# A SwiGLU layer's stream from another queue, and its sums in the ring of the weights

## The chip, the cores and the metric

The kernel runs on one core of a Trainium2 chip. The metric is the device time of one execution in microseconds (us); the median of a few runs is taken. The engines are named as in the profile: PE is TensorE's matmul (PEld its weight load), DVE is VectorE, ACT is ScalarE, POOL is GpSimd, SP is SyncE, which issues most DMAs. Each engine works through its own instructions in order and waits on semaphores for the others.

## The reference

One encoder layer over 1024 positions of width 1024 in float32: a half-step SwiGLU, a mixing part (latent attention beside RWKV-7 heads), a second half-step SwiGLU and a norm. What the change touches is in the two SwiGLUs:

```python
h = x
u = modulate(rmsnorm(h, ffn1_norm_g[l]), sh1, sc1)
h = h + 0.5 * gt1[:, None, :] * swiglu(u, ffn1_w_gate[l], ffn1_w_up[l], ffn1_w_down[l])
...
def swiglu(u, w_gate, w_up, w_down):
    return (jax.nn.silu(u @ w_gate) * (u @ w_up)) @ w_down
```

The hidden width is 2816, which is 22 tiles of 128.

## The kernel before

**Products.** Each float32 operand is split into a high and a low part (`split`, L60): ACT copies the high one (L61), DVE subtracts it to get the low one (L62). A product is then three matmuls, high by high, high by low, low by high (`mm3`, L68), issued in that order, so the first two of a product need only ACT's copy and the third needs DVE's subtraction as well. Both parts of an operand lie in one tile `pair` of 4 KB per partition. The pairs of the weights come from a ring of eight tiles with the tag `"wo"`: the n-th takes the place of the (n-8)-th, and places are handed out in the order in which the Python code asks for them.

**The SwiGLU** (`ffn`) has two stages. The product up goes over the hidden tiles two at a time (f = 0, 2, ..., 20). For f of 2 and more, `products7` makes a 2x2 block product with seven products in place of eight, once for the gate and once for up: 2 x 7 products of 12 matmuls, 168 matmuls of 128x512 for each f. Between them DVE builds sums of weights (L376, L397), adds parts of results (L487, L492) and multiplies gate by up (L493), and ACT copies partial results out of PSUM (L390). The two hidden tiles `c` of an f go to DRAM (`hidD`, L497). From f = 4 on, `sums` also makes three differences of them, T3, T2 and T4, on DVE (L505: four subtractions, one of them in place on `c`), and stores them (`sumD`, L507). They need the result of the last of the f's fourteen products. The product down reads hidD and sumD back (`hraw`, L545), splits them, makes the seven products in groups (`seven_products`), and `give` (L560) adds each result to the stream `h`.

**The stream.** `h` is eight tiles d of 128 rows by two halves a of 512 positions, 256 KB each. During the product up its room is lent out: to the hidden tiles `c` (tags `h0_0` to `h6_0`), and to a ring of scratch tiles, `k.spare`, from which `tmp` takes in turn (T, t, part and hraw among others). At the turn from up to down the stream is read again, from `x` in the first SwiGLU (L1675, called from `turn`) and from `hD` in the second, by 16 DMAs on SP's queue, a = 0 first and d in order. `turn(-1)` comes before the last f and sets the scratch ring that this f and the product down use; `turn(0)` starts the stream's loads.

**Order.** A scheduler orders each engine's instructions from the code, within what tiles and semaphores allow. A tile that is asked for is given out only after all that was asked for before it in the same ring. While the first SwiGLU goes up, DVE also does `mod` steps (L140, L143, with weights `wmod`) and some `trig` steps, put in between the products.

Of the kernel before, what the change touches and what calls it, by code (L numbers as in the profile page):

```python
# [13 lines left out]
F32 = mybir.dt.float32  # L14
# [8 lines left out]
P = 128  # L23
D = 1024
S = 1024
HB = 512
ND = D // P
# [43 lines left out]
def banks(k, **names):  # L71

    for n, b in names.items():
        turn = itertools.cycle(b)
        k.bank.update((x, turn) for x in n.split("_"))
# [7 lines left out]
def tmp(k, name, n=HB, dt=F32):  # L83

    pool, tag, size = next(k.spare if n == HB else k.wide)
    return pool.tile([P, size], dt, name=name, tag=tag)[:, :n]


def spare(slots):

    return itertools.cycle([(*s, D)[:3] for s in slots])
# [196 lines left out]
def empty():  # L288
    return [[None, None] for _ in range(ND)]
# [13 lines left out]
def h_tiles(k, pool, a, out, singles=0):  # L303

    for d in range(singles):
        out[d][a] = pool.tile([P, HB], F32, name=f"h{d}_{a}", tag=f"h{d}_{a}")
    for d in range(singles, ND, 2):
        t = pool.tile([P, 2, HB], F32, name=f"h{d}_{a}", tag=f"h{d}_{a}")
        out[d][a], out[d + 1][a] = t[:, 0], t[:, 1]


def norm_raw(k, r, x, d, name, sh):

    nc = k.nc
    g, b = k.gs[name][:, d : d + 1], k.mod[:, sh, d : d + 1]
    if d % 2:
        nc.gpsimd.tensor_tensor(out=x, in0=x, in1=r[1], op=ALU.mult)
        nc.scalar.activation(out=x, in_=x, func=AF.Identity, scale=g, bias=b)
    else:
        nc.vector.scalar_tensor_tensor(out=x, in0=x, scalar=g, in1=r[0], op0=ALU.mult, op1=ALU.mult)  # L320
        nc.scalar.activation(out=x, in_=x, func=AF.Identity, bias=b)
# [42 lines left out]
def products7(k, pool, w, f, u, sink):  # L364


    nc = k.nc
    A = []
    for i in range(2):
        raw = pool.tile([P, 2, HB], F32, name="raw", tag="raw", bufs=4)  # L370
        nc.sync.dma_start(out=raw.rearrange("p a (d q) -> p (a d) q", q=P), in_=w[f + i])
        A.append((raw[:, 0], raw[:, 1]))
    (a11, a12), (a21, a22) = A

    def sub(x, y, out):
        nc.vector.tensor_tensor(out=out, in0=x, in1=y, op=ALU.subtract)  # L376
        return out

    def product(x, name, onto=None):
        hi, lo = pair(pool, "wo", 8)  # L380
        split(k, x, hi, lo)
        t = ps(k, "w7") if onto is None else onto
        for i in range(4):
            c = slice(i * P, (i + 1) * P)
            mm3(k, t, hi[:, c], lo[:, c], *u[name][i], onto is None and i == 0, i == 3, onto is not None)
        return t

    def kept(x):
        t = tmp(k, "part")
        nc.scalar.copy(out=t, in_=x)  # L390
        return t

    x = product(a11, "11")
    m1 = kept(x)
    yield
    s1 = pool.tile([P, HB], F32, name="s1", tag=next(k.s1))
    nc.vector.tensor_tensor(out=s1, in0=a21, in1=a22, op=ALU.add)  # L397
    y = product(s1, "T1")
    yield
    s3 = sub(a11, a21, a21)  # L400
    s2 = sub(s1, a11, a11)
    u2 = kept(product(s2, "T2", x))
    yield
    sink(0, 0, product(a12, "21"), m1)
    yield
    u3 = kept(product(s3, "T3", x))
    sink(1, 1, y, u3)
    yield
    sink(1, 0, product(a22, "T4"), u3)
    yield  # L410
    s4 = sub(a12, s2, a12)
    sink(0, 1, product(s4, "22", y), u2)
    yield
# [20 lines left out]
def ffn(  # L434
    k, u, h, wg, wu, wd, gt, pool, groups, cells, start, turn, steps1, steps2, final, done, pieces, ahead=None
# [6 lines left out]
    nc = k.nc  # L442
# [4 lines left out]
    def cell():  # L447
        where, tag = next(cells)
        return where.tile([P, 2, HB], F32, name="c", tag=tag)
# [31 lines left out]
    def up(f):  # L481

        c = [None, None]

        def silu(i, j, x, y):
            c[i] = cell() if c[i] is None else c[i]
            nc.vector.tensor_tensor(out=c[i][:, j], in0=x, in1=y, op=ALU.add)  # L487
            nc.scalar.activation(out=c[i][:, j], in_=c[i][:, j], func=AF.Silu)  # L488

        def gated(i, j, x, y):  # L490
            t = tmp(k, "t")
            nc.vector.tensor_tensor(out=t, in0=x, in1=y, op=ALU.add)  # L492
            nc.vector.tensor_tensor(out=c[i][:, j], in0=c[i][:, j], in1=t, op=ALU.mult)  # L493
            if (i, j) == (0, 1) and f >= NPL:
                sums()
            if (i, j) in ((1, 0), (0, 1)):
                nc.sync.dma_start(out=hidD[f + i], in_=c[i])  # L497

        def sums():

            (b11, b12), (b21, b22) = ((x[:, 0], x[:, 1]) for x in c)

            def sub(x, y, name=None):
                out = tmp(k, name) if name else x
                nc.vector.tensor_tensor(out=out, in0=x, in1=y, op=ALU.subtract)  # L505
                if name:
                    nc.sync.dma_start(out=sumD[name, f], in_=out)  # L507
                return out

            sub(b22, b12, "T3")  # L510
            t2 = sub(b22, sub(b12, b11), "T2")
            sub(b21, t2, "T4")

        return products7(k, pool, wg, f, u, silu), products7(k, pool, wu, f, u, gated)
# [1134 lines left out]
def tile_layer(ctx, tc, I, out):  # L1649
    k = Ctx()  # L1650
    setup(ctx, k, tc, I, out)
    nc = k.nc
# [10 lines left out]
    with pool_("ffn1") as pool:  # L1663
        fs = [(pool, f"f{i}") for i in range(12)]
        h0, h1 = [(pool, f"h{d}_0") for d in range(0, ND, 2)], [(pool, f"h{d}_1", HB) for d in range(6)]
        wide = [(pool, "e"), (pool, "h6_1")]
        k.wide = spare(us)
        k.spare = spare(fs[8:])
        h = empty()
        u = {}  # L1670

        def load_x(a):
            h_tiles(k, pool, a, h, 6 * a)
            for d in range(ND):
                nc.sync.dma_start(out=h[d][a], in_=I["x"][d, :, a * HB : (a + 1) * HB])  # L1675

        vectors(k, pool)
        load_x(0)
        early = 2
        slices = {}  # L1680
# [38 lines left out]
        def normed(a, r):  # L1719
            for d in range(ND):  # L1720
                if a == 0 and d >= early:
                    mods(d)
                norm_raw(k, r, h[d][a], d, "ffn1_norm_g", 0)
            return [h[d][a] for d in range(ND)]
# [4 lines left out]
        x = []  # L1729

        def first_half():
            spread_c(k, pool)
            load_mods(range(early, 4))
            load_x(1)
            load_mods(range(4, ND))
            x.append(normed(0, r0))
            stream_first(k, u, x[0], slots)
# [8 lines left out]

        def turn(g):
            if g < 0:
                k.spare = spare(wide + h1)
                return  # L1750
            if g == 0:
                banks(k, dn="67012345")
                for a in range(2):
                    load_x(a)
            if g == 3:
                banks(k, in0="012", dn_in1="34", in2="5", norm="67")
                k.spare = spare(fs[8:])
# [20 lines left out]
        def ahead(a, tiles):  # L1778
# [6 lines left out]
        ffn(  # L1785
            k, u, h, I["ffn1_w_gate"], I["ffn1_w_up"], I["ffn1_w_down"], k.mod[:, 2, :], pool, groups(fs, us),
            itertools.chain([wide[0], us[7]], itertools.cycle(h0)), (lambda: None, lambda: (first_half(), second_half()), lambda: None, both), turn, steps1, steps2,
            n2.final, n2.done, [(0, WHOLE), (1, WHOLE)], ahead,
        )
# [71 lines left out]
    h, y, u = empty(), empty(), {}  # L1861
    own = lambda name, side="right": ctx.enter_context(pool_(name, side))
    h0, h1 = [f"h{d}_0" for d in range(0, ND, 2)], [(f"h{d}_1", HB) for d in range(6)]
    up = Pools((own("u3b"), [f"u{i}" for i in range(8)]))
    pool = Pools((own("h2b"), h0), (own("w2"), ("raw", "f8", "f9", "f10", "f11", "nwy", "nwt")))
    us, fs = [(up, f"u{i}") for i in range(16)], [(pool, f"f{i}") for i in range(12)]
    h0, h1 = [(pool, t) for t in h0], [(pool, *t) for t in h1]
# [11 lines left out]
    es = [(pool, "e"), (pool, "e2")]  # L1879
    k.spare = spare(es)  # L1880
    slots = iter(fs + us)
    x = []

    def then(a, r):
        for d in range(ND):
            norm_raw(k, r, h[d][a], d, "ffn2_norm_g", 6)
        x.append([h[d][a] for d in range(ND)])
        if a == 0:
            stream_first(k, u, x[0], slots)
        else:  # L1890
            stream_second(k, u, x[1], us[8:])
# [14 lines left out]

    def turn(g):
        if g < 0:
            k.spare = spare(es + h1)
            return  # L1910
        if g == 0:
            banks(k, dn="67012345")
            for a in range(2):
                h_tiles(k, pool, a, h, 6 * a)
                for d in range(ND):
                    nc.sync.dma_start(out=h[d][a], in_=k.hD[a][:, d, :])
        if g == 3:
            banks(k, dn="670123", norm="45")
            k.spare = spare(us[8:])
# [61 lines left out]
```

## Time and profile before

| | |
|---|---|
| median of three runs | 2087.97 us (2081.59 to 2088.29) |
| profiled execution | 2091.08 us, its span 2089.0 us |
| mean granted clock of TensorE | 0.978 |
| PE busy | 1992.1 us, 95% of the span |
| DVE, ACT, POOL busy | 1542.5, 885.2, 242.0 us |
| matmuls of the product up (`ps_w`) | 3744, 873.8 us |

The span runs from the first to the last instruction. The granted clock is 1.00 where TensorE has its full 2.4 GHz and 0.50 where it has 1.2 GHz. A busy time counts an engine as busy while an instruction is in it; the mean duration of a single matmul (near 395 ns) is longer than the distance between two, since they are pipelined.

### The profile page before, as it was taken

What the parts mean: (1) busy time and instruction counts of PE and PEld (TensorE: products, weight loads), DVE (VectorE), ACT (ScalarE), POOL (GpSimd) and SP (SyncE); (2) the same over time, 40 slices, a digit from 0 to 9 for tenths busy, and PEclk for the clock granted to TensorE, in tenths of its full rate; (3) what the DMA queues carried; (4) which work ended last, traced back from release to release, by engine and by line L of the source; (5) the groups of instructions that cost most, each with busy time, mean ns of one, the idle gap of its engine ahead of it and who ended that gap; (6) DMA issues with size and microseconds to landing.
All of it is one profiled execution on the core that took longest, in us unless ns stands there. A gap on an engine that the chain in (4) does not pass through costs nothing.

```text
span 2089.0 us, 29462 instructions
## 1 busy us (share of the span) xinstructions
PE 1992.1 (95%) x10648; PEld 1605.8 (77%) x10648; DVE 1542.5 (74%) x2955; ACT 885.2 (42%) x1662; POOL 242.0 (12%) x271
## 2 busy tenths in 40 slices
PE   6999999998999999998988999899999999989998
PEld 4788888886888777766767787787888888868887
DVE  6999997668996577887655667567566656689975
ACT  5643334344443465543343434355333333344433
POOL 1100000000000244531141221111000000000001
PEclk8999999999999999999988999999999999999999
DMA  8277743246452124666347884741223323474412
GB/s 335 85 246 249 247 172 126 101 172 227 152 171 86 66 66 120 154 149 147 89 100 155 190 186 133 237 159 42 87 79 106 121 76 107 162 251 152 141 61 81
DMA packets 225681, 302.12 MB, mean 145 GB/s; under 512 B 104704, under 2 KB 138880, under 8 KB 225536
## 3 DMA queue, kind: packets, MB, share of 16 engines
q1 hardware_dynamic: 219600, 294.84, 45.3%
q0 software_dynamic: 1280, 3.15, 0.5%
q10 hardware_dynamic: 4656, 2.25, 0.4%
q8 instruction: 84, 1.38, 0.3%
q14 instruction: 61, 0.50, 0.1%
HBM read 216.81 MB, written 80.74 MB: 142 GB/s over the span
## 4 chain that ended last, share of the span: by engine, by line
PE 77%; DVE 12%; DMA 5%; issue 3%; ACT 2%; POOL 1%; SPq 1%; DVEq 0%; ACTq 0%; POOLq 0%
PE ps_w L68 39%; PE ps_dn L68 19%; PE ps_in L68 5%; PE ps_wo L68 4%; DVE pair L62 2%; PE ps_ov L1264 2%; PE ps_s L68 1%; DVE T L1359 1%; DVE Tpr L1355 1%; PE ps_z L1472 1%; PE ps_y L1506 1%; PE ps_pt L1256 1%; DVE wmod L140 1%; DMA hraw<-hidD 1%; DMA fD<-T 1%
## 5 line engine op out<-in xcount | busy, mean ns | idle before, releaser
L68 PE MATMUL ps_w<-pair 128*128 128x512 f32 x3744 | 873.8, 395 | 12.8 <-ACT pair L61 9.4
L68 PEld LDWEIGHTS ps_w<-pair 128*128 128x128 f32 x3744 | 704.6, 189 | 179.1 <-ACT pair L61 10.7
L68 PE MATMUL ps_dn<-pair 128*128 128x512 f32 x1512 | 357.5, 398 | 15.1 <-DVE h L560 11.8
L68 PEld LDWEIGHTS ps_dn<-pair 128*128 128x128 f32 x1512 | 287.7, 191 | 84.0 <-DVE h L560 13.5
L68 PE MATMUL ps_in<-pair,win 128*128 128x512 f32 x960 | 241.0, 403 | 2.6 <-ACT pair L282 2.2
L61 ACT CAST pair<-raw 128x512 fp32r<-128x512 f32 x256 | 153.6, 621 | 183.5 <-PE ps_w L68 98.2
L68 PEld LDWEIGHTS ps_in<-pair,win 128*128 128x128 f32 x960 | 179.5, 190 | 51.7 <-issue 10.4
L62 DVE TENSOR_TENSOR pair<-raw,pair 128x512 fp32r<-128x512 f32 x256 | 175.1, 696 | 38.8 <-ACT pair L61 38.7
L560 DVE SCALAR_TENSOR_TENSOR h<-ps_dn,mod,h 128x512 f32<-128x512 f32 (+1 forms) x208 | 148.7, 725 | 53.4 <-PE ps_dn L68 49.5
L390 ACT COPY part<-ps_w 128x512 f32<-128x512 f32 x120 | 70.4, 587 | 207.8 <-PE ps_w L68 196.7
L61 ACT CAST pair<-draw 128x256 fp32r<-128x256 f32 x216 | 80.1, 404 | 135.6 <-PE ps_dn L68 64.3
L61 ACT CAST pair<-hraw 128x512 fp32r<-128x512 f32 x142 | 86.1, 619 | 65.9 <-PE ps_dn L68 41.5
L62 DVE TENSOR_TENSOR pair<-hraw,pair 128x512 fp32r<-128x512 f32 x142 | 95.5, 683 | 11.8 <-ACT pair L61 11.4
L492 DVE TENSOR_TENSOR t<-ps_w,part 128x512 f32<-128x512 f32 x80 | 53.8, 685 | 56.9 <-ACT part L390 46.8
L208 POOL TENSOR_TENSOR nacc<-nacc,nsq 128x512 f32<-128x512 f32 x12 | 18.1, 1508 | 660.8 <-ACT nsq L204 660.8
L62 DVE TENSOR_TENSOR pair<-draw,pair 128x256 fp32r<-128x256 f32 x216 | 84.9, 416 | 11.5 <-ACT pair L61 11.4
L140 DVE SCALAR_TENSOR_TENSOR wmod<-wmod,cact 128x1024 f32<-128x1024 f32 x68 | 82.6, 1216 | 4.7 <-DMA wmod<-w_mod 4.7
L68 PE MATMUL ps_dn<-pair,dh 128*128 128x512 f32 (+1 forms) x320 | 83.8, 350 | 0.0
L487 DVE TENSOR_TENSOR c<-ps_w,part 128x512 f32<-128x512 f32 x80 | 53.4, 684 | 39.7 <-ACT part L390 33.5
L703 POOL TENSOR_TENSOR h<-h,nr 128x256 f32<-128x256 f32 (+1 forms) x6 | 5.4, 920 | 650.0 <-ACT nr L231 650.0
L68 PE MATMUL ps_wo<-pair,woh 128*128 128x512 f32 x256 | 80.6, 396 | 0.0
L488 ACT ACTIVATE c<-c 128x512 f32<-128x512 f32 x80 | 49.3, 631 | 31.6 <-DVE c L487 30.7
(349 smaller groups left out, 2798.6 us busy)
## 6 DMA issues: line engine op xcount, KB each, us to landing
wmod<-w_mod SPq DMA_DIRECT2D x68, 512.0 KB, 4.6
raw<-ffn_w_gate SPq DMA_DIRECT2D x44, 512.0 KB, 4.3
raw<-ffn_w_up SPq DMA_DIRECT2D x44, 512.0 KB, 4.3
hidD<-c SPq DMA_DIRECT2D x44, 512.0 KB, 3.3
draw<-ffn_w_down SPq DMA_DIRECT2D x44, 512.0 KB, 5.3
hraw<-hidD SPq DMA_DIRECT2D x72, 256.0 KB, 3.4
h<-x SPq DMA_DIRECT2D x32, 256.0 KB, 5.2
hD<-h SPq DMA_DIRECT2D x32, 256.0 KB, 2.0
```

The source lines that it names most:

```text
L61: k.nc.scalar.copy(out=hi, in_=src)
L62: k.nc.vector.tensor_tensor(out=lo, in0=src, in1=hi.bitcast(F32), op=ALU.subtract)
L68: k.nc.tensor.matmul(out, lhsT=x, rhs=y, start=start, stop=stop, skip_group_check=onto)
L140: k.nc.vector.scalar_tensor_tensor(out=w, in0=w, scalar=1.0, in1=k.cact, op0=ALU.mult, op1=ALU.mult, accum_out=m)
L390: nc.scalar.copy(out=t, in_=x)
L487: nc.vector.tensor_tensor(out=c[i][:, j], in0=x, in1=y, op=ALU.add)
L488: nc.scalar.activation(out=c[i][:, j], in_=c[i][:, j], func=AF.Silu)
L492: nc.vector.tensor_tensor(out=t, in0=x, in1=y, op=ALU.add)
L560: nc.vector.scalar_tensor_tensor(out=y, in0=x, scalar=gt[:, d : d + 1], in1=y, op0=ALU.mult, op1=ALU.add)
L1256: nc.tensor.transpose(tp[:, q : q + P], pr[:, s0 + q : s0 + q + P], k.ident)
L1264: nc.tensor.matmul(x.po[:, cols], lhsT=pt[:, b * P : (b + 1) * P], rhs=k.v[b][:, cols], start=b == 0, stop=b == x.i)
L1355: nc.vector.tensor_tensor(out=v, in0=T[:, t, 0:m][:, None, :].broadcast_to([P, n, m]), in1=xp[:, t, m:][:, :, None].broadcast_to([P, n, m] ...
```

## The change

Three edits in both SwiGLUs. The stream's 16 loads at the turn are issued from POOL, four tiles of d at a time, in the order (d 0, 1; a 0), (d 0, 1; a 1), (d 2, 3; a 1), (d 2, 3; a 0), then the same for d 4 to 7. T3, T2 and T4 no longer come from the scratch ring: for each f from 4 on `sums` asks the ring `"wo"` for two tiles of 4 KB, one for T3 and T2, one for T4. And the scratch ring of the last f and the product down takes the tiles of `h1` in another order.

```diff
+def stream_again(k, pool, h, src):
+
+    for a in range(2):
+        h_tiles(k, pool, a, h, 6 * a)
+    for q in range(0, ND, 4):
+        for i, a in ((0, 0), (0, 1), (2, 1), (2, 0)):
+            for d in range(q + i, q + i + 2):
+                k.nc.gpsimd.dma_start(out=h[d][a], in_=src(d, a))
...
             (b11, b12), (b21, b22) = ((x[:, 0], x[:, 1]) for x in c)
 
+            t, t4 = (pool.tile([P, 2, HB], F32, name="T", tag="wo", bufs=8) for _ in range(2))
+            place = {"T3": t[:, 0], "T2": t[:, 1], "T4": t4[:, 0]}
+
             def sub(x, y, name=None):
-                out = tmp(k, name) if name else x
+                out = place[name] if name else x
                 nc.vector.tensor_tensor(out=out, in0=x, in1=y, op=ALU.subtract)
...
             if g < 0:
-                k.spare = spare(wide + h1)
+                k.spare = spare(wide + [h1[i] for i in (4, 5, 0, 2, 3, 1)])
                 return
             if g == 0:
                 banks(k, dn="67012345")
-                for a in range(2):
-                    load_x(a)
+                stream_again(k, pool, h, x_half)
```

The second SwiGLU has the same edits, with `hD` in place of `x`. In the changed kernel the lines of the product up stand ten to thirteen further on: the multiplication by up is L503, the subtractions of T are L518.

**Between two f of the product up.** The rows below are PE's at the end of f = 12 of the second SwiGLU, and the same rows stand at each such place. A name is out<-in, `ps_w7` is a result in PSUM, `pair` the operands, and x3 means three matmuls in a row. Before, `ps_w7_14727` is the last product of f = 12:

```order
L68 MATMUL ps_w7_14910<-pair_12487,pair_14907 128x512 x2
L68 MATMUL ps_w7_14727<-pair_12870,pair_14819 128x512 x3
L68 MATMUL ps_w7_14727<-pair_12871,pair_14819 128x512 x3
L68 MATMUL ps_w7_14727<-pair_12872,pair_14819 128x512 x3
L68 MATMUL ps_w7_14727<-pair_12873,pair_14819 128x512 x3
L68 MATMUL ps_w7_14855<-pair_13102,pair_14890 128x512 x3
L68 MATMUL ps_w7_14855<-pair_13103,pair_14890 128x512 x3
L68 MATMUL ps_w7_14855<-pair_13104,pair_14890 128x512 x3
L68 MATMUL ps_w7_14855<-pair_13105,pair_14890 128x512 x3
L68 MATMUL ps_w7_14910<-pair_12487,pair_14907 128x512
```

The products 14910 and 14855 belong to the next f; 14910 has begun before the last product of f = 12 has. In the changed kernel the last product is `ps_w7_14714`, and nothing of the next f stands ahead of its end:

```order
L68 MATMUL ps_w7_14714<-pair_12863,pair_14806 128x512 x3
L68 MATMUL ps_w7_14714<-pair_12864,pair_14806 128x512 x3
L68 MATMUL ps_w7_14841<-pair_12474,pair_14838 128x512 x2
L68 MATMUL ps_w7_14861<-pair_13097,pair_14858 128x512 x2
L68 MATMUL ps_w7_14841<-pair_12474,pair_14838 128x512
L68 MATMUL ps_w7_14841<-pair_12475,pair_14838 128x512 x3
```

The next f now begins with two products of which two matmuls each (high by high, high by low) come first; the fifth matmul is the first that takes a low part, that of pair_14838.

At the same place DVE has these rows in the kernel before (`t` is the sum read from the last product's PSUM):

```order
L492 TENSOR_TENSOR t_14834<-ps_w7_14727,part_14757 128x512
L62 TENSOR_TENSOR pair_15024<-raw_14982,pair_15024 128x512
L493 TENSOR_TENSOR c_14641<-c_14641,t_14834 128x512
L505 TENSOR_TENSOR T3_14837<-c_14661,c_14641 128x512
L505 TENSOR_TENSOR c_14641<-c_14641 128x512
L505 TENSOR_TENSOR T2_14841<-c_14661,c_14641 128x512
L62 TENSOR_TENSOR pair_15041<-raw_14982,pair_15041 128x512
L505 TENSOR_TENSOR T4_14844<-c_14661,T2_14841 128x512
L487 TENSOR_TENSOR c_14923<-ps_w7_14910,part_14868 128x512
```

And in the changed kernel these:

```order
L502 TENSOR_TENSOR t_14821<-ps_w7_14714,part_14744 128x512
L503 TENSOR_TENSOR c_14628<-c_14628,t_14821 128x512
L518 TENSOR_TENSOR T_14824<-c_14648,c_14628 128x512
L518 TENSOR_TENSOR c_14628<-c_14628 128x512
L518 TENSOR_TENSOR T_14824<-c_14648,c_14628 128x512
L518 TENSOR_TENSOR T_14825<-c_14648,T_14824 128x512
L62 TENSOR_TENSOR pair_14838<-raw_14834,pair_14838 128x512
L62 TENSOR_TENSOR pair_14858<-s1_14856,pair_14858 128x512
```

The low part that PE's fifth matmul takes (pair_14838) has moved behind all of the sums; before, the low parts of the next f's first products stand ahead of them. This order holds at all 16 places between two f, eight in each SwiGLU (f = 4 to 18). At 13 of them DVE has just the seven instructions from `t` to that low part; in the first SwiGLU four, three and no `mod` multiplications and no, no and three `trig` steps stand among them at f = 4, 6 and 8.

**At the turn.** The same rows of the changed kernel at the end of f = 20 of the first SwiGLU; `hraw` are hidden tiles read back for the product down, and pair_3944 is the first weight of it, 256 wide:

```order
L502 TENSOR_TENSOR t_3836<-ps_w7_3635,part_3684 128x512
L62 TENSOR_TENSOR pair_4024<-hraw_4022,pair_4024 128x512
L62 TENSOR_TENSOR pair_4063<-hraw_4061,pair_4063 128x512
L503 TENSOR_TENSOR c_3702<-c_3702,t_3836 128x512
L62 TENSOR_TENSOR pair_4098<-hraw_4096,pair_4098 128x512
L518 TENSOR_TENSOR T_3839<-c_3741,c_3702 128x512
L518 TENSOR_TENSOR c_3702<-c_3702 128x512
L62 TENSOR_TENSOR pair_4131<-hraw_4129,pair_4131 128x512
L518 TENSOR_TENSOR T_3839<-c_3741,c_3702 128x512
L62 TENSOR_TENSOR pair_4136<-hraw_4134,pair_4136 128x512
L62 TENSOR_TENSOR pair_4172<-hraw_4170,pair_4172 128x512
L518 TENSOR_TENSOR T_3840<-c_3741,T_3839 128x512
```

The low part of pair_3944 is DVE's next row. PE has eight matmuls between the last product up and the first that takes this low part. Before, ten matmuls of the product down stand ahead of the last product up. The second SwiGLU's turn reads alike.

## Rows read from the trace of the kernel before

**Rows 1.** Busy time by stretch: us, PE, PEld, DVE, ACT, POOL, PEclk, DMA share, GB/s.
```profile
100.00:150.00 50.00, 50.00 (x220) 40.92 (x219) 47.26 (x94) 19.34 (x35) 0.00 (x0) 1.00 0.72 243
...
400.00:450.00 50.00, 50.00 (x220) 40.91 (x219) 32.67 (x52) 17.20 (x31) 0.00 (x0) 1.00 0.30 107
...
1550.00:1600.00 50.00, 50.00 (x217) 40.37 (x216) 30.54 (x48) 17.78 (x31) 0.00 (x0) 1.00 0.29 100
```

**Rows 2.** PE's matmuls of the product up by line, 100 to 450, then 1450 to 1850.
```profile
L68 PE MATMUL ps_w<-pair 128*128 128x512 f32 x1524 | 350.4, 392 | 0.2 <-ACT part L390 0.2
...
L68 PE MATMUL ps_w<-pair 128*128 128x512 f32 x1692 | 392.7, 393 | 0.0
```

**Rows 3.** DVE in order of time between two f: start us, us, what.
```profile
1577.12 0.68 DVE L492 TENSOR_TENSOR t<-ps_w,part 128x512 f32<-128x512 f32 x1
1577.72 0.68 DVE L62 TENSOR_TENSOR pair<-raw,pair 128x512 fp32r<-128x512 f32 x1
1578.32 0.69 DVE L493 TENSOR_TENSOR c<-c,t 128x512 f32<-128x512 f32 x1
1579.04 0.69 DVE L505 TENSOR_TENSOR T<-c 128x512 f32<-128x512 f32 x1
1579.77 0.69 DVE L505 TENSOR_TENSOR c<-c 128x512 f32<-128x512 f32 x1
1580.49 0.69 DVE L505 TENSOR_TENSOR T<-c 128x512 f32<-128x512 f32 x1
1581.10 0.68 DVE L62 TENSOR_TENSOR pair<-raw,pair 128x512 fp32r<-128x512 f32 x1
1581.70 0.68 DVE L505 TENSOR_TENSOR T<-c,T 128x512 f32<-128x512 f32 x1
```

**Rows 4.** DVE's groups, 100 to 480: count | busy us, mean ns | idle before.
```profile
L140 DVE SCALAR_TENSOR_TENSOR wmod<-wmod,cact 128x1024 f32<-128x1024 f32 x54 | 65.7, 1217 | 4.7 <-DMA wmod<-w_mod 4.7
...
L746 DVE SCALAR_TENSOR_TENSOR trig<-trig 128x512 f32<-128x512 f32 x20 | 13.4, 683 | 0.0
```

**Rows 5.** PE in order of time at the first turn: idle before it in brackets.
```profile
499.31 6.66 PE L68 MATMUL ps_dn<-pair 128*128 128x512 f32 x21 [3.34 <-DVE h L560]
510.49 4.84 PE L68 MATMUL ps_dn<-pair 128*128 128x512 f32 x13 [4.51 <-DVE h L560]
```

**Rows 6.** PE in stretches of one us behind the first of these: us, PE, PEclk, DMA.
```profile
500.00:501.00 1.00, 1.00 (x5) 0.75 1.01 414
501.00:502.00 1.00, 1.00 (x4) 0.50 1.02 410
502.00:503.00 1.00, 1.00 (x4) 0.50 0.95 240
503.00:504.00 1.00, 1.00 (x4) 0.54 0.81 274
504.00:505.00 1.00, 1.00 (x6) 1.00 1.00 383
```

**Rows 7.** The turns by stretch, columns as in the first group.
```profile
470.00:495.00 25.00, 25.00 (x111) 20.48 (x110) 24.11 (x49) 14.42 (x32) 0.00 (x0) 1.00 0.83 267
495.00:515.00 20.00, 12.15 (x39) 9.02 (x38) 14.69 (x30) 4.71 (x11) 0.00 (x0) 0.83 0.75 257
...
1860.00:1880.00 20.00, 12.76 (x41) 9.30 (x40) 13.90 (x29) 3.94 (x10) 0.00 (x0) 0.83 0.79 270
```

**Rows 8.** The chain that ended last, at the first turn: start us, us, what.
```profile
496.17 8.28 DMA T2D<-T
...
504.51 5.15 DMA h<-x
...
509.68 0.76 DVE h L560
```

**Rows 9.** DMA issues: queue, count, KB each, us to landing.
```profile
h<-x SPq DMA_DIRECT2D x32, 256.0 KB, 5.2
...
ybD<-lgx POOLq DMA_DIRECT2D x8, 256.0 KB, 4.2
```

More of the change, by code (lines that the diff above doesn't have):

```diff
@@ L1670, in tile_layer @@
         u = {}
+        x_half = lambda d, a: I["x"][d, :, a * HB : (a + 1) * HB]
         def load_x(a):
@@ L1674, in load_x @@
             for d in range(ND):
-                nc.sync.dma_start(out=h[d][a], in_=I["x"][d, :, a * HB : (a + 1) * HB])
+                nc.sync.dma_start(out=h[d][a], in_=x_half(d, a))
         vectors(k, pool)
@@ L1908, in turn @@
         if g < 0:
-            k.spare = spare(es + h1)
+            k.spare = spare(es + [h1[i] for i in (4, 5, 0, 2, 3, 1)])
             return
@@ L1912, in turn @@
             banks(k, dn="67012345")
[L1913 to L1916, printed above, removed]
+            stream_again(k, pool, h, lambda d, a: k.hD[a][:, d, :])
         if g == 3:
```

## The prediction, on record before the run

> **What bounds the kernel now.** The first view is busy time by stretch. Over both products up PE is busy 50.00 us of 50, with 217 to 220 matmuls and a granted clock of 1.00, while DVE stands between 30.5 us (second SwiGLU) and 47.3 us (first, with its mod steps) [rows 1]. The groups by line say the same from the other side: from 100 to 450 us PE was idle 0.2 us in 1524 matmuls, from 1450 to 1850 us 0.0 in 1692 [rows 2]. So these stretches, some 750 us of the span, are bound by PE alone, at 0.2273 to 0.2304 us a matmul (50 over 220 and 217), and an idle microsecond that is put into them is one more microsecond of the end. What the reader is to look for is therefore not busy time but whether PE still finds its next operand ready.
>
> The second view is PE in order of time at the turn from up to down. There it does wait: 3.34 us and 4.51 us in the first SwiGLU, for DVE's addition to the stream [rows 5], which the chain leads back to a load of the stream (5.15 us) and that to the store of T2 in a scratch tile on the stream's place (8.28 us) [rows 8]. In 20 us of the first turn PE is idle 20 - 12.15 = 7.9 us and the clock is 0.83, which is 0.17 x 20 = 3.4 us of full speed lost; in the second 7.2 and 3.4 [rows 7]. So the two turns lose 11.3 + 10.6 = 21.9 us together. That is all that the change can win there.
>
> **The change, part by part.**
>
> *T's room in the ring of the weights.* No operation is added: four subtractions, three stores as before. What changes is which of PE's operands must wait. The places of the ring are given out in the code's order, and the code asks for T's two tiles after the last product of an f and ahead of the next f's first weight. So a weight of the next f can't get its place before T has one, and the orders shown with the change are the result: the next f's first low part stands on DVE behind t, c, T3, c, T2 and T4, and t needs the end of the f's last product. Before, PE had begun the next f by then.
>
> The length of that chain is read from the same seven instructions of before [rows 3]. Where an instruction needs the one before it, starts lie 0.72 us apart (1578.32, 1579.04, 1579.77, 1580.49); where it doesn't, 0.60 (1580.49, 1581.10, 1581.70). From t to T4 are five such needs, 5 x 0.72 = 3.6; from T4 to the low part 0.60; it lasts 0.68: 4.9 us. For the hand-over from PE to DVE and back I add 0.1 each, an estimate after the one place where it shows (DVE's addition ends at 509.68 + 0.76 = 510.44, PE starts at 510.49 [rows 5, 8]). PE has four matmuls that need high parts only, 4 x 0.23 = 0.9. Idle: 4.9 + 0.2 - 0.9 = 4.2 us. Bounds: 3.5 if all starts lie 0.60 apart, 4.7 with hand-overs of 0.35.
>
> There are 16 such places. Thirteen have the bare chain: 13 x 4.2 = 54.6 us. At f = 4 and 6 of the first SwiGLU four and three mod multiplications of 1.22 us [rows 4] stand in the chain, and the others' starts are then 0.60 apart (4.3 in place of 4.9): 4.3 + 4 x 1.22 + 0.2 - 0.9 = 8.5 and 7.3. At f = 8 three trig steps of at most 0.68 [rows 4]: between 4.2 and 5.6, taken as 5.1. Idle in all: 75.5 us. Nothing gives it back, since PE alone bounds what follows.
>
> *The clock behind the idle time.* After the idle 3.34 us of the first turn, PE's next stretches of one us had granted clocks of 0.75, 0.50, 0.50 and 0.54, then 1.00 again [rows 5, 6]: the lower level, 1.2 GHz, for a loss of 0.25 + 0.50 + 0.50 + 0.46 = 1.7 us. The idle 4.2 us lies between that one and the 4.51 us, whose stretch counts 13 matmuls in its first 4.84 us [rows 5], where full speed has 21. So I charge 1.7 us at each of the 16 places: 27.2 us. The bound on the other side is nothing, if four matmuls and an idle stretch are not like a longer idle one.
>
> *The turn.* The last f's T delay the first weight of the product down as well. From t to its low part are thirteen DVE instructions, six of them splits of hidden tiles, so starts lie 0.60 apart: 12 x 0.60 + 0.4 (256 wide, taken as somewhat over half of 0.68) = 7.6, + 0.2, less eight matmuls, 1.8: 6.0 idle, and 1.7 for the clock. If the stream is there in time, this 7.7 us takes the place of 11.3 and 10.6: 6.5 us won in two turns. The new order and the scratch tiles are worth that only if T's stores no longer stand ahead of the loads, which holds: their tiles are not the stream's. Bounds: nothing won, or 21.9.
>
> *POOL's queue.* POOL is free (0.00 busy in all of these stretches [rows 1, 7]), so nothing is queued behind the loads that others wait for. A load from it has its row in ybD, as large, 4.2 us to landing against 5.2 for the stream's own [rows 9]; I cost it at nothing, up to 1 us either way.
>
> *The sum.* 75.5 + 27.2 - 6.5 = 96 us on the profiled 2091.1, so 2187; the median of the runs lies 3.1 below that execution, so 2184. Scheduling also shifts the mixing part's order a little; no row prices that, and I give it nothing, with some 6 us either way.
>
> **Rivals.**
>
> *The idle time doesn't bring the clock down* (0.14). For it: the four matmuls run in the middle of the wait. Against: the idle 3.34 us was enough [rows 5, 6]. Then 75.5 + 12.0 - 21.9 = 66 us: 2154.
>
> *The stream starves* (0.07). DVE is busy 24.11 us of the 25 before the turn [rows 7], and loads from POOL would wait for a free DVE, so behind the chain. 16 x 256 KB at the 410 GB/s of [rows 6] are 10.2 us, and with the clock 12 us more at each turn: 2208. Against it: ybD's 4.2 us. It decides only if the loads start after T4. The Trainium skill, "SBUF — State Buffer", in the box on the "DVE blocks DMA" trap, says that a DMA issued from GpSimd has its descriptors written by GpSimd, which a VectorE operation in a two-port mode locks out. That page speaks for this rival and against the change; the rows show no load from POOL beside a full DVE, so the trace doesn't settle it.
>
> *The change is a repair of the turn alone* (0.03): PE finds products to run while T is made, as before, and the stream is early. Then all that the turns lose is won: 2088 - 21.9 = 2066. It decides where DVE's chain ends ahead of PE's own work, under 0.9 us, and the chain is 4.9.
>
> *The loads win nothing* (in the forecast's 0.72): 2191.
>
> The rest (0.04) is what I don't see, in the mixing part above all.
>
> **How the numbers follow.** The likeliest is the sum, 2184 us (0.72; its own range 2170 to 2200, from 3.7 to 4.7 us of idle time a place and a turn between nothing and 12 us won). The range goes down to the rival without the clock and up to the one with the starved stream: 2150 to 2210. A time within 0.3% (6 us) can't be told from no change here. Slower by more: 0.95; faster: 0.03; within: 0.02.
>
> **What would show it.** In the trace after: PE idle 4 us before the first low parts of each f, ended by DVE's L62, 16 times, 3.5 to 5 us each and more at f = 4 and 6; stretches with a granted clock of 0.50 behind each; T3 to T4 on DVE directly before that L62; 217 to 220 matmuls in 50 us become some 190. At the turn: one wait of some 6 us for the first weight's low part in place of two for the stream. The prediction is wrong if PE has no such waits, if the clock stays at 1.00 behind them, or if PE waits for the stream's loads behind the turn.

## The result and the profile after

| | before | changed |
|---|---|---|
| median | 2086.16 us | 2253.36 us |
| span of the profiled execution | 2089.0 us | 2249.8 us |
| mean granted clock | 0.978 | 0.950 |

The ratio is 1.080 (95% interval 1.078 to 1.082): 8% slower, where 2184 us and at most 2210 were predicted. The sign and the place were right; the loss is 161 us of span where 96 were worked out.

PE in order of time over the first places between two f in the changed kernel (start us, us, instructions, idle before them and what ended it):

```profile
162.97 6.71 PE L68 MATMUL ps_w<-pair 128*128 128x512 f32 x28 [1.06 <-DVE c L497]
183.28 31.72 PE L68 MATMUL ps_w<-pair 128*128 128x512 f32 x128 [13.60 <-DVE pair L62]
217.50 7.38 PE L68 MATMUL ps_w<-pair 128*128 128x512 f32 x24 [2.49 <-DVE c L497]
228.00 5.54 PE L68 MATMUL ps_w<-pair 128*128 128x512 f32 x16 [3.13 <-DVE t L502]
244.27 37.61 PE L68 MATMUL ps_w<-pair 128*128 128x512 f32 x152 [10.73 <-DVE pair L62]
283.46 3.02 PE L68 MATMUL ps_w<-pair 128*128 128x512 f32 x12 [1.58 <-DVE t L502]
293.25 41.45 PE L68 MATMUL ps_w<-pair 128*128 128x512 f32 x172 [6.76 <-ACT pair L61]
338.80 41.58 PE L68 MATMUL ps_w<-pair 128*128 128x512 f32 x168 [4.09 <-DVE pair L62]
384.46 36.80 PE L68 MATMUL ps_w<-pair 128*128 128x512 f32 x152 [4.08 <-DVE pair L62]
422.71 3.95 PE L68 MATMUL ps_w<-pair 128*128 128x512 f32 x16 [1.46 <-DVE t L502]
...
573.53 121.89 PE L68 MATMUL ps_dn<-pair 128*128 128x512 f32 x522 [10.01 <-ACT pair L61]
```

Where before PE waited 0.2 us in all of this stretch [rows 2], it now waits once for each f. From f = 10 on the wait is 4.08 to 4.10 us, the bare one; so it is at all eight places of the second SwiGLU. In front of them stand 13.60, 10.73 and 6.76 us. And there are short waits for `t` or `c` inside an f, which the prediction did not have. The last row is the turn: 10.01 us.

The groups by line of the changed kernel (busy, mean ns, idle before, releasers) give the sum:

```profile
L68 PE MATMUL ps_w<-pair 128*128 128x512 f32 x3744 | 921.4, 408 | 117.1 <-DVE pair L62 80.3
...
L68 PE MATMUL ps_dn<-pair 128*128 128x512 f32 x1512 | 354.4, 396 | 20.3 <-ACT pair L61 20.2
```

The product up has 117.1 us of idle time where it had 12.8, and its matmuls take 921.4 us where they took 873.8: 104.3 + 47.6 us. The product down adds 5.2 of idle time (20.3 against 15.1) less 3.1 of busy (354.4 against 357.5). That is 154.0 of the span's 160.8; the rest, 6.8, lies in the mixing part, which the change doesn't touch, and in the ends.

One bare wait as DVE saw it, the end of an f in the second SwiGLU of the changed kernel:

```profile
1812.28 0.69 DVE L502 TENSOR_TENSOR t<-ps_w,part 128x512 f32<-128x512 f32 x1 [1.37 <-PE ps_w L68]
1813.00 0.69 DVE L503 TENSOR_TENSOR c<-c,t 128x512 f32<-128x512 f32 x1
1813.73 0.69 DVE L518 TENSOR_TENSOR T<-c 128x512 f32<-128x512 f32 x1
1814.45 0.69 DVE L518 TENSOR_TENSOR c<-c 128x512 f32<-128x512 f32 x1
1815.18 0.69 DVE L518 TENSOR_TENSOR T<-c 128x512 f32<-128x512 f32 x1
1815.90 0.69 DVE L518 TENSOR_TENSOR T<-c,T 128x512 f32<-128x512 f32 x1
1816.51 0.68 DVE L62 TENSOR_TENSOR pair<-raw,pair 128x512 fp32r<-128x512 f32 x1
```

The seven instructions run without a gap, 1812.28 to 1817.19, 4.9 us, and PE starts again at 1817.25. Behind it PE in stretches of one us (us, PE, PEclk, DMA share, GB/s):

```profile
1816.00:1817.00 1.00, 0.00 (x0) 0.50 1.05 416
1817.00:1818.00 1.00, 0.75 (x2) 0.50 0.98 375
1818.00:1819.00 1.00, 1.00 (x4) 0.50 0.67 260
...
1821.00:1822.00 1.00, 1.00 (x4) 0.50 0.00 0
1822.00:1823.00 1.00, 1.00 (x4) 0.66 0.00 0
1823.00:1824.00 1.00, 1.00 (x6) 1.00 0.74 184
```

The clock is at its lower level, 1.2 GHz, from before PE starts again until some 5.4 us later, a loss of 0.38 + 4 x 0.50 + 0.34 = 2.7 us. In the kernel before the fall behind the idle 3.34 us cost 1.7 [rows 6].

The 13.60 us at f = 4, again on DVE:

```profile
172.12 0.69 DVE L503 TENSOR_TENSOR c<-c,t 128x512 f32<-128x512 f32 x1
172.72 0.15 DVE L143 TENSOR_TENSOR mod<-mod,b_mod 128x1 f32<-128x1 f32 x1
174.76 1.23 DVE L140 SCALAR_TENSOR_TENSOR wmod<-wmod,cact 128x1024 f32<-128x1024 f32 x1 [1.89 <-DMA wmod<-w_mod]
...
175.91 0.69 DVE L518 TENSOR_TENSOR T<-c 128x512 f32<-128x512 f32 x1
...
177.77 1.23 DVE L140 SCALAR_TENSOR_TENSOR wmod<-wmod,cact 128x1024 f32<-128x1024 f32 x1 [0.44 <-DMA wmod<-w_mod]
...
180.79 1.23 DVE L140 SCALAR_TENSOR_TENSOR wmod<-wmod,cact 128x1024 f32<-128x1024 f32 x1 [1.11 <-DMA wmod<-w_mod]
...
182.54 0.68 DVE L62 TENSOR_TENSOR pair<-raw,pair 128x512 fp32r<-128x512 f32 x1
```

The mod steps inside the chain don't only take their 1.2 us, they wait for their weights first, 1.89 + 0.44 + 1.11 us in this piece. DVE's group of L140 was idle 4.7 us for such loads before [rows 4], and 18.6 us now. At f = 6 such a wait stands ahead of `t` as well and holds up the start of the chain. At f = 8 no mod step stands in it, but trig steps do, on DVE and on ACT; there PE's wait ends with ACT's copy of the next f's first weight, which stands behind three trig instructions of ACT:

```profile
233.73 1.23 DVE L140 SCALAR_TENSOR_TENSOR wmod<-wmod,cact 128x1024 f32<-128x1024 f32 x1 [1.26 <-DMA wmod<-w_mod]
234.88 0.69 DVE L502 TENSOR_TENSOR t<-ps_w,part 128x512 f32<-128x512 f32 x1
...
291.96 0.72 ACT L768 ACTIVATE trig<-trig,halfpi 128x512 f32<-128x512 f32 x1
292.59 0.60 ACT L61 CAST pair<-raw 128x512 fp32r<-128x512 f32 x1
```

At the turn, the chain that ended last in the changed kernel (start us, us, what):

```profile
562.98 0.61 DVE c L503
563.59 1.28 DVE pair L62 x2
564.87 0.03 DVE t L502
564.90 7.03 DMA hraw<-T4D
571.93 0.02 issue
571.95 1.53 ACT pair L61 x3
573.49 0.04 issue
573.53 26.55 PE ps_dn L68 x108
```

The same pattern: behind `t` a hidden tile must be read back (7.03 us) and split by ACT before the product down's first weight has its turn there. So PE waits for ACT's copy of that weight, its high part, and the low part follows on DVE when PE already runs:

```profile
573.08 1.01 ACT L61 CAST pair<-draw 128x256 fp32r<-128x256 f32 x3
...
574.41 1.09 DVE L62 TENSOR_TENSOR pair<-draw,pair 128x256 fp32r<-128x256 f32 x3
```

### The profile page after: what moved, and what is told of

Its sections match the earlier page's. It is cut to its first block, busy times and chain, and to the rows that moved or that the text cites. A ratio compares the mean times of both kernels' runs of the same rounds, so it can differ in the third digit from the quotient of the medians.

```text
span 2249.8 us, 29446 instructions
## 1 busy us (share of the span) xinstructions
PE 2040.1 (91%) x10648; PEld 1633.3 (73%) x10648; DVE 1549.9 (69%) x2955; ACT 882.0 (39%) x1662; POOL 259.4 (12%) x303
## 4 chain that ended last, share of the span: by engine, by line
PE 67%; DVE 17%; DMA 8%; issue 3%; ACT 2%; POOL 1%; SPq 0%; DVEq 0%; ACTq 0%; POOLq 0%
PE ps_w L68 34%; PE ps_dn L68 19%; PE ps_in L68 4%; PE ps_wo L68 3%; DMA wmod<-w_mod 2%; DVE pair L62 2%; DVE wmod L140 2%; DVE T L518 1%; PE ps_ov L1277 1%; PE ps_s L68 1%; DMA vu<-vD 1%; DVE Tpr L1368 1%; DVE t L502 1%; DVE T L1372 1%; PE ps_z L1485 1%
## 5 line engine op out<-in xcount | busy, mean ns | idle before, releaser
L68 PE MATMUL ps_w<-pair 128*128 128x512 f32 x3744 | 921.4, 408 | 117.1 <-DVE pair L62 80.3
L68 PEld LDWEIGHTS ps_w<-pair 128*128 128x128 f32 x3744 | 732.5, 197 | 303.6 <-DVE pair L62 89.3
L68 PE MATMUL ps_dn<-pair 128*128 128x512 f32 x1512 | 354.4, 396 | 20.3 <-ACT pair L61 20.2
L140 DVE SCALAR_TENSOR_TENSOR wmod<-wmod,cact 128x1024 f32<-128x1024 f32 x68 | 83.1, 1223 | 18.6 <-DMA wmod<-w_mod 18.4
L407 DVE TENSOR_TENSOR s<-raw 128x512 f32<-128x512 f32 x40 | 27.6, 691 | 59.9 <-DMA raw<-ffn_w_up 37.8
L319 POOL DMA_DIRECT2D h<-x x16 | 8.7, 547 | 505.2 <-DVE pair L62 458.0
```

Of the source, the lines that this page charges most:

```text
L68: k.nc.tensor.matmul(out, lhsT=x, rhs=y, start=start, stop=stop, skip_group_check=onto)
L140: k.nc.vector.scalar_tensor_tensor(out=w, in0=w, scalar=1.0, in1=k.cact, op0=ALU.mult, op1=ALU.mult, accum_out=m)
```

## The experiments

All ratios are against the kernel before, from runs on the same chip.

| kernel | median us | ratio (95%) |
|---|---|---|
| T in the weights' ring, alone | 2238.0 | 1.074 (1.072 to 1.076) |
| changed, T back in scratch | 2084.7 | 1.000 (0.999 to 1.002) |
| loads from POOL, alone | 2096.0 | 1.005 (1.004 to 1.007) |
| changed, T in a ring of its own | 2075.1 | 0.995 (0.993 to 0.997) |
| changed, PE's wait filled | 2235.5 | 1.072 (1.070 to 1.075) |
| changed, no loads of mod weights | 2240.1 | 1.075 (1.072 to 1.078) |
| own ring, loads from SP | 2067.5 | 0.992 (0.990 to 0.994) |
| before, T in a ring of its own | 2067.3 | 0.992 (0.990 to 0.994) |
| changed, no mod steps | 2226.5 | 1.066 (1.062 to 1.069) |
| changed, last T in scratch | 2227.7 | 1.068 (1.065 to 1.070) |

**One edit alone, and all but it.** First the kernel before with T's place changed and nothing else:

```diff
+            t, t4 = (pool.tile([P, 2, HB], F32, name="T", tag="wo", bufs=8) for _ in range(2))
+            place = {"T3": t[:, 0], "T2": t[:, 1], "T4": t4[:, 0]}
...
-                out = tmp(k, name) if name else x
+                out = place[name] if name else x
```

> The kernel before with one edit alone: T3, T2 and T4 take places in the ring of the weights. Theory (the ring's order makes the next f's first low part wait for T): nearly the whole loss, 2235 to 2260 us, PE idle some 4.1 us at 13 places between two f and more at f = 4 and 6 of the first SwiGLU. Rival (the loss comes from the stream's loads on POOL's queue or from the order of the scratch tiles): 2080 to 2100 us.

2238.0 us, 153 above the kernel before on the same chip, where the changed kernel was 167 above. PE's bare waits are there with 4.08 and 4.09 us. Then the changed kernel without this edit:

```diff
-            t, t4 = (pool.tile([P, 2, HB], F32, name="T", tag="wo", bufs=8) for _ in range(2))
-            place = {"T3": t[:, 0], "T2": t[:, 1], "T4": t4[:, 0]}
...
-                out = place[name] if name else x
+                out = tmp(k, name) if name else x
```

> The changed kernel with T3, T2 and T4 back in the scratch ring; loads from POOL and the new order of the scratch tiles stay. Theory: no wait between two f, so 2070 to 2092 us, by what the turn still loses. Rival (loads or scratch order cost the time): 2200 us or more.

2084.7, no change from before. The place of T is the loss, and the rival that puts it on the loads or the scratch order falls. The 15 us between the first of these kernels and the changed one are not at the turns (10.7 and 10.4 us of wait there, against 10.0 and 10.1); the stretch from the first product down's end to the second product up's start is 669.2 us in the one and 683.7 in the other, and 677.2 before. No edit is there; only the scheduler's order differs. What in it costs the 15 us was not followed.

The kernel with T back isn't quite the kernel before: its product down is idle 7.6 us where that one had 15.1, though the medians are the same. It differs from the next kernel, which has the loads from POOL alone (2096.0 us, product down idle 15.9), only in the order of the scratch tiles. So beside POOL's loads that order is worth some 11 us; by itself it was not run.

**The loads alone.** The kernel before with the loads from POOL in the new order (the function of the diff above, called from `turn`), T and the scratch order left:

> The kernel before with the stream's loads from POOL's queue in the new order, nothing else. Theory: 2075 to 2095 us; T's stores still stand ahead of loads that want their scratch tiles, so the turn is won at most in part. Rival (loads from POOL start late because DVE is busy at the turn): 2100 to 2115 us, with PE waiting for the stream.

2096.0 us, half a per cent slower, between the two. The product down is idle 15.9 us (15.1 before): nothing is won at the turn, since T's scratch tiles still lie on the stream's place. The chain there goes through T3's store (2.73 us) and then the load from POOL:

```profile
492.80 2.73 DMA T3D<-T
...
496.16 8.04 DMA h<-x
...
504.22 0.76 DVE h L570
```

**The ring, not the place.** The changed kernel with the eight tiles shared out as six for the weights and two for T:

```diff
-            t, t4 = (pool.tile([P, 2, HB], F32, name="T", tag="wo", bufs=8) for _ in range(2))
+            t, t4 = (pool.tile([P, 2, HB], F32, name="T", tag="T", bufs=2) for _ in range(2))
...
-        hi, lo = pair(pool, "wo", 8)
+        hi, lo = pair(pool, "wo", 6)
```

> The changed kernel with the same room shared out otherwise: six places for the weights, and two places of a ring of their own for T (where eight weight tiles are needed at once, the last two take T's). Theory (order in one ring, not the place or its size): no wait of 4 us between two f, 2065 to 2095 us. Rival (DVE's four subtractions behind the last product cost the time wherever T lies, or six places are too few): 2150 us or more.

2075.1 us: half a per cent faster than the kernel before. The instructions and the room in all are the same; how it is shared out, and with that the order in which it is given out, differs, and the 4.1 us are gone. The rival (DVE's subtractions cost the time wherever T lies) falls.

**The clock.** The changed kernel with 17 matmuls more at each place, on the first high part, for nobody:

```diff
+        if name == "11" and fill and f - 2 >= NPL:
+            spent = ps(k, "norm")
+            for i in range(17):
+                nc.tensor.matmul(spent, lhsT=hi[:, :P], rhs=u["11"][0][0], start=i == 0, stop=i == 16)
```

> The changed kernel with 17 matmuls added at the head of each f from 6 on, into a PSUM tile that nobody reads, so that PE works through the wait for the first low part (17 x 0.23 = 3.9 of the idle 4.1 us). Theory: the wait itself stays, but the granted clock no longer falls behind it; the changed kernel's matmuls of the product up took 47.6 us more than before, and some 40 of that come back: 2203 to 2220 us. Rival (they are slow for another reason, or the added matmuls only push the rest back): 2245 us or more.

2235.5 us, between the two. PE over 200 us of the second SwiGLU, the changed kernel first, then the filled one (us, PE busy, PEclk, DMA share, GB/s):

```profile
1600.00:1800.00 200.00, 180.72 (x736) 0.94 0.24 85
```

```profile
1600.00:1800.00 200.00, 193.29 (x826) 1.00 0.24 85
```

The clock no longer falls there, and an f that took 47.4 us from place to place (1769.87 to 1817.25) takes 45.1 (1673.13 to 1718.19): 2.3 us a place. The second SwiGLU's product up is 16.0 us shorter (512.2 from its first matmul to the first of the product down, against 528.2). The first SwiGLU's is not: the product down starts there at 573.92 us, in the changed kernel at 573.53. At f = 4 and 6 the added 4 us did not fill the wait, which still is 10.2 us each behind them, and the wait of 1.46 us for `t` stands at each of the first SwiGLU's last five f now, where the changed kernel had it at two. That is why the total gains 18 us and not 40. The clock's cost at a bare place is shown, net of what the added matmuls cost. What the fall takes in all can be summed in the changed kernel: PE's busy time in stretches of 1 us, times what the granted clock lacks of 1.00, is 22.4 us in the first product up (from 90 us on) and 20.6 in the second, 43.0 of the 47.6 us. In the kernel before it is 0.0 in both.

**The mod steps.** The changed kernel with the multiplications of the mod steps left, and their loads gone:

```diff
-            loaded.append(mod_loads(k, v, d))
+            loaded.append(tmp(k, "wmod", D))
...
-        mod_one(k, v, d, loaded[i])
+        mod_one(k, v, d, loaded[i], k.cact)
```

> The changed kernel without the loads of the later modulation weights: the same multiplications on DVE, but of c with itself, so what the layer is scaled by is left out. Theory (at f = 4 and 6 the chain on DVE holds mod steps that wait for their loads): PE's idle time at the first places falls from 13.6 and 10.7 us to the 8.5 and 7.3 that the instructions alone make, the short waits near them go, 2225 to 2240 us. Rival (it is DVE's own time): no change, 2247 to 2260 us.

2240.1 us, at the edge of the theory's range, and the trace doesn't bear out its reason: DVE's mod steps wait for nothing now, and yet the first place is 19.05 us. The scheduler set ten of the multiplications between `t` and the low part where four had stood (170.93 to 186.11 us on DVE), 12.3 us of work:

```profile
187.37 37.52 PE L68 MATMUL ps_w<-pair 128*128 128x512 f32 x152 [19.05 <-DVE pair L62]
```

So this one leaves open how the excess divides between loads and work. The next takes both out:

```diff
-        for v, d, _ in todo[len(loaded) : i + 2]:
-            loaded.append(mod_loads(k, v, d))
         v, d, then = todo[i]
-        mod_one(k, v, d, loaded[i])
+        k.nc.vector.tensor_copy(out=k.mod[:, v, d : d + 1], in_=k.bmod[:, v * ND + d : v * ND + d + 1])
```

> The changed kernel without the later mod steps' loads and multiplications (a copy of the bias stands in, so the layer's later scales are left out). Theory (what stands at f = 4, 6 and 8 beyond the bare wait is mod work and its loads inside the chain): PE's waits between 160 and 300 us, 39.4 us together in the changed kernel, become three bare ones of 4.1 us and a 1.5 or two, so some 24 us less, with the clock 2218 to 2232 us. Rival (the first places wait for something else, the weights' loads for one): 2240 us or more.

2226.5 us, 27 less than the changed kernel. PE's waits between 160 and 300 us are 16 us together, 23 less, about as expected, and the first places are bare:

```profile
173.34 37.55 PE L68 MATMUL ps_w<-pair 128*128 128x512 f32 x152 [4.16 <-DVE pair L62]
212.35 3.94 PE L68 MATMUL ps_w<-pair 128*128 128x512 f32 x16 [1.46 <-DVE t L500]
220.39 37.92 PE L68 MATMUL ps_w<-pair 128*128 128x512 f32 x152 [4.09 <-DVE pair L62]
```

What stood there beyond the bare wait at f = 4 and 6 was mod work with its loads, taken together. At f = 8 the wait is bare as well (4.10 us), though no mod step stood in that chain: without the mod steps DVE has done the last trig step by 145 us, so that those too are gone from it.

**The turn.** The changed kernel with T of the last f alone back in the scratch ring:

```diff
-            t, t4 = (pool.tile([P, 2, HB], F32, name="T", tag="wo", bufs=8) for _ in range(2))
-            place = {"T3": t[:, 0], "T2": t[:, 1], "T4": t4[:, 0]}
+            place = {}
+            if f < NF - 2:
+                t, t4 = (pool.tile([P, 2, HB], F32, name="T", tag="wo", bufs=8) for _ in range(2))
+                place = {"T3": t[:, 0], "T2": t[:, 1], "T4": t4[:, 0]}
```

> The changed kernel with T of the last f alone back in the scratch ring. Theory (at the turn the product down's first weight waits for the last T, whose chain holds the splits of hidden tiles that wait for their loads): the two waits of 10 us become those of the kernel with T back, 7.6 us in all; 2236 to 2246 us. Rival (the 10 us are the late hidden tiles or the stream themselves): 2249 us or more.

2227.7 us, 26 less, more than expected. The product down's idle time falls from 20.3 to 6.0 us, its first ten matmuls again run ahead of the last products up (552.12), and the waits of 10 us are gone. The other places keep theirs. In the profiled executions the span is 22.5 us shorter, of which 5.0 lie in the mixing part (678.7 us against 683.7 from the first product down's end to the second product up's start), so 17.5 belong to the two SwiGLUs. The product down has 14.3 us of them as idle time and 1.9 as busy time; in the products up 4.8 less of busy time stand against 3.7 more of idle time. The median lies 8 us below the expected range; the 5 us of the mixing part, which no edit touches, are in that.

**What beats both.** T in a ring of its own, with the new order of the stream's loads, but from SP:

```diff
-                k.nc.gpsimd.dma_start(out=h[d][a], in_=src(d, a))
+                k.nc.sync.dma_start(out=h[d][a], in_=src(d, a))
```

> The kernel with T in a ring of its own, its stream loads in the new order but from SP's queue. Theory (the place of T and the order of loads make the gain, not the queue): 2070 to 2082 us. Rival (SP's queue is held by stores and loads ahead of them, so the stream comes late): 2083 to 2100 us, with waits of PE for the stream at the turn.

2067.5 us, below the expected range. And the kernel before with T in that ring and nothing else:

> The kernel before with T in a ring of its own (six places for weights) and nothing else. Theory (T's stores no longer stand ahead of the stream's loads): 2072 to 2084 us. Rival (the order of the loads is needed too, or six places cost something): 2084 to 2100 us.

2067.3 us, 0.992 of before, also below its range, the fastest of all, tied with the one above it: neither the new order of loads nor POOL's queue adds anything once T is off the stream's place. With POOL's queue it is 2075.1; the intervals of the two ratios touch (0.993 to 0.997, 0.990 to 0.994), so that the queue's own price is at most some 8 us and not settled. PE at the first turn of the fastest kernel waits for nothing:

```profile
471.52 8.56 PE L68 MATMUL ps_w<-pair 128*128 128x512 f32 x36
479.92 25.38 PE L68 MATMUL ps_dn<-pair 128*128 128x512 f32 x110
```

Before, the same place had 3.34 and 4.51 us [rows 5], both for additions that waited for a load of the stream, the second of them behind T2's store [rows 8]. Its product down has lost 15.1 us of idle and 8.0 of busy time (349.5 against 357.5): 23.1 us, near the 21.9 that the prediction worked out as the most that the turns could give.

## Why the prediction was right and wrong

**The bound and the mechanism: right.** What failed are sizes: the four terms below were too small or left out, all on the same side. PE alone bounds the products up, and T's place in the ring makes the next f's first low part wait. The experiments with that edit alone, without it, and with a ring of its own show it. The bare wait was worked out at 4.2 us and is 4.09, 13 times.

**The mod and trig steps: mis-sized.** The term for f = 4, 6 and 8 had 8.5, 7.3 and 5.1 us, 20.9 together; they are 13.60, 10.73 and 6.76, 31.1, with 8.3 us of short waits beside them (1.06, 2.49, 3.13, 1.58). The step that failed is "four and three mod multiplications of 1.22 us ... stand in the chain": it priced an instruction in the chain by its duration alone. Such an instruction brings its own waits into the chain: at f = 4 they are 3.4 of the 5.1 us that are missing there. One that stands ahead of `t` delays the start, as at f = 6. At f = 8 the three trig steps were priced on DVE alone, and PE's wait ended with ACT. The 4.7 us that the mod group was idle for its loads stood in the row that was read [rows 4]; while nothing waited for DVE there, that cost nothing. Missing: 18.5 us. Without the mod steps the time falls by 27, which holds the part that was forecast too.

**Inside an f: left out.** Eight waits of 1.46 us for `t`, 11.7 us. The last product adds onto a PSUM tile that `t` must have read. While products of the next f were at hand PE did these meanwhile; without them it waits here as well. The prediction followed the missing cover only to the end of the f.

**The clock: mis-sized.** 1.7 us at each place, 27.2 together; the product up's matmuls take 47.6 us more. Of these 43.0 are the clock, 2.7 a place on average, and at a bare place the rows after show 2.7, since the lower level lasts 5.4 us of work there. The filled kernel gave back 2.3 a place. The other 4.6 us are not the clock; the last matmul ahead of a wait counts its whole 0.39 us as busy, where the next would start after 0.23, and at some 28 waits that makes 4.5, an estimate. The 1.7 was read behind waits of 3.34 and 4.51 us at the turn (in the kernel before it is 1.7 behind either) and carried over to another pattern of work and wait, because 4.2 lies between the two. Only nothing was set as the other bound; one above it was missing. The rival without a fall (0.14) is ruled out by the rows. Its premise fails too: the four matmuls run directly behind the last product (16 in one piece, 1809.17 to 1813.17), not in the middle of the wait.

**The turn: wrong in sign.** 6.5 us were to be won; the product down is 2.1 us worse (5.2 idle less 3.1 busy), so 8.6 are missing. "From t to its low part are thirteen DVE instructions, six of them splits of hidden tiles, so starts lie 0.60 apart" failed for the reason of the mod steps: the splits wait for their tiles, and from `t` (564.78) to the low part (574.41) DVE takes 9.6 us in place of 12 x 0.60 = 7.2. And PE could not run the eight matmuls that were taken off, since the weight's high part was late as well: on ACT it stands behind the split of a hidden tile whose load took 7.03 us. The wait is 10.0 us in place of 6.0.

**The rest.** 18.5 + 11.7 + 20.4 + 8.6 = 59.2, with 6.8 for the mixing part and the ends and 1.4 less for the bare places (53.2 in place of 54.6): 64.6, which is the 160.8 of span that were measured less the 96.2 that were worked out (75.5 + 27.2 - 6.5).

**The rival of a starved stream: not seen.** The loads from POOL landed in 4.8 us (x) and 4.6 us (hD) in the changed kernel, and 5.1 and 4.8 from SP at the turns before:

```profile
h<-x POOLq DMA_DIRECT2D x16, 256.0 KB, 4.8
h<-hD POOLq DMA_DIRECT2D x16, 256.0 KB, 4.6
```

PE waited for none of them. In the kernel with T in its own ring they landed in 6.1 and 5.9 us from POOL, 5.2 and 5.8 from SP. Single ones took longer, 8.04 us in the kernel with the loads alone; what held it is not shown. The box on the "DVE blocks DMA" trap of the Trainium skill's page "SBUF — State Buffer" speaks of an operation in a two-port mode, which a full DVE by itself is not. DVE's rows at the turn are TENSOR_TENSOR and SCALAR_TENSOR_TENSOR; no run here tells whether they run in such a mode, and none shows a load from POOL held up in that way.

## What to carry to other kernels

A ring of tiles is also an order: who asks last waits for all who asked before, so a tile that is filled late doesn't belong in the ring from which the bounding engine's operands come; two smaller rings of the same room gave 0.8%, the shared one cost 7%. When an engine's chain becomes critical, price each instruction in it with what it waits for, not with its duration alone, and look for the other waits that the lost cover had hidden too. A fall of the clock is priced by a row with the same pattern of work and wait, or with a bound on each side.

## What the hardware showed beyond expectation

Behind the bare waits of 4.1 us with four matmuls before them TensorE ran at 1.2 GHz for 5.4 us of work (1817.25 to some 1822.7), longer than behind the 3.34 us of before (some 3.4 us [rows 6]) and behind the 4.51 us (3.4 too). Here the granted clock had fallen while PE was still idle (0.50 from 1816 on). Before, it fell only when PE had started again: some 1.2 us later behind the 3.34 us (start at 499.31, 0.75 in the stretch from 500 to 501) and some 0.25 us later behind the 4.51 (start at 510.49, 0.87 from 510 to 511). So the length of the wait alone doesn't give its price. Seventeen matmuls without a purpose in that wait kept the granted clock at 1.00 and made each f 2.3 us shorter.
